# Weight gradient on one core: six phases over eight PSUM banks, slice 0 through hardware queues, results stored from SP

## The chip, the cores and the metric

The kernel runs on one core of a Trainium2 chip. The metric is the device time of one launch in microseconds. The kernel before takes 190.88 us (median of three runs, 190.75 to 191.67).

## What is computed

```python
batch, m, k, n = 16, 512, 1024, 768
input:       (batch, m, k) float32
grad_output: (batch, m, n) float32

grad_weight = np.einsum('bmk,bmn->kn', input, grad_output)   # (1024, 768) float32
```

Batch and m together are 8192 rows that are summed over. The result is X^T G with X of 8192 x 1024 and G of 8192 x 768.

## The kernel before

The 8192 rows are cut into 64 slices of 128 rows (one row for each partition). The 1024 columns of X are eight blocks of 128, numbered k = 0 to 7; the 768 columns of G are a wide part of 512 and a narrow part of 256. One slice therefore needs 16 matmuls: for each k a wide one (128x512, one PSUM bank of 2 KB a partition) and a narrow one (128x256). Over 64 slices that is 512 wide and 512 narrow matmuls, in bf16 with float32 accumulation.

**Loads.** All loads stand on the queue of GpSimd (POOL), which rounds float32 to bf16 on the way. Slice 0 comes in four DMAs (`load_first_slice`, L77 to L80: wide G, two halves of X, narrow G), slice 1 in three (L91 to L93), and slices 2 to 63 in 31 pairs of two DMAs, first G (384 KB in bf16, L107), then X (512 KB, L108). A pair is usable when its X has landed. POOL has eight completion semaphores for its DMAs, taken in turn, so that a DMA is issued only when the one eight places earlier has landed. X and G have 18 buffers each for pairs.

**Order of the work on PE.** The slices fall into chunks of 4, 6, 9, 12, 16 and 17 (`CHUNKS`). Within a chunk, PE takes each slice as it comes and does six of its wide matmuls (seven in the first chunk) into open banks (L209, tiles `st`). The rest of a chunk, two wide blocks and eight narrow ones, is its backlog: it is done group by group during the next chunk (`do_backlog_group`, L151, tile `pb`), two groups before the next chunk's first slice and the others spread between its slices. A program written out in this order is what PE runs; it never changes it. So between two slices of a chunk PE has backlog to do, for data that landed long ago. Warm-up matmuls on a constant tile run ahead of the first slice and four short ones behind each of the first eight slices (L61).

**Adding up.** At a chunk's end the banks are copied (first chunk) or added into `acc` in SBUF: three banks by one DVE add each (L230, L232), a backlog group by one add (L162) or, in the second chunk, a copy on ACT (L160).

**Stores.** Eleven DMAs on POOL's queue: six wide blocks in one DMA of 1536 KB (L234), then each group of the last backlog, two wide and eight narrow, as it is added (L164).

Of the kernel before, what the change touches and what calls it, by code (L numbers as in the profile page):

```python
# [1 line left out]

# [4 lines left out]

CHUNKS = [4, 6, 9, 12, 16, 17]
R_MAIN = 2
WARMUP_MM = 8
FILLER_MM = 4
FILLER_SLICES = 8


@with_exitstack
def kernel(
# [4 lines left out]
    out: bass.AP,  # L24
):
    nc = tc.nc
    P = 128

    B, M, K = input.shape
    _, _, N = grad_output.shape  # L30
    BM = B * M
    S = BM // P
    KSUB = K // P
    NA = 512
    NB = N - NA

    assert sum(CHUNKS) == S

    bf16 = mybir.dt.bfloat16
    f32 = mybir.dt.float32  # L40
# [5 lines left out]
    x_pool = ctx.enter_context(tc.tile_pool(name="x_pool", bufs=18))  # L46
    g_pool = ctx.enter_context(tc.tile_pool(name="g_pool", bufs=18))
    acc_pool = ctx.enter_context(tc.tile_pool(name="acc_pool", bufs=1))
    warm_pool = ctx.enter_context(tc.tile_pool(name="warm_pool", bufs=1))
    ps_pool = ctx.enter_context(tc.tile_pool(name="ps_pool", bufs=2, space=bass.MemoryType.PSUM))  # L50
    pb_pool = ctx.enter_context(tc.tile_pool(name="pb_pool", bufs=2, space=bass.MemoryType.PSUM))
# [5 lines left out]
    wps = pb_pool.tile([P, NA], f32, name="pb")

    def dummy_matmuls(count, width):
        for i in range(count):  # L60
            nc.tensor.matmul(  # L61
                wps[:, :width],
                warm[:, 0:P],
                warm[:, 0:width],
                start=(i == 0),
                stop=(i == count - 1),
            )

    dummy_matmuls(WARMUP_MM, NA)

    slice_aps = [None] * S

    def load_first_slice():
        xa = x_pool.tile([P, NA], bf16, name="xta", bufs=1)
        xb = x_pool.tile([P, NA], bf16, name="xtb", bufs=1)
        gt = g_pool.tile([P, N], bf16, name="gt1", bufs=2)
        nc.gpsimd.dma_start(out=gt[:, 0:NA], in_=G[0:P, 0:NA])  # L77
        nc.gpsimd.dma_start(out=xa, in_=X[0:P, 0:NA])  # L78
        nc.gpsimd.dma_start(out=xb, in_=X[0:P, NA:K])  # L79
        nc.gpsimd.dma_start(out=gt[:, NA:N], in_=G[0:P, NA:N])  # L80
        xparts = [xa, xa, xa, xa, xb, xb, xb, xb]

        def x_ap(k):
            return xparts[k][:, (k % 4) * P : (k % 4 + 1) * P]

        slice_aps[0] = (x_ap, gt)

    def load_single_slice(s):
        xt = x_pool.tile([P, K], bf16, name="xt1", bufs=1)
        gt = g_pool.tile([P, N], bf16, name="gt1", bufs=2)  # L90
        nc.gpsimd.dma_start(out=gt[:, 0:NA], in_=G[s * P : (s + 1) * P, 0:NA])  # L91
        nc.gpsimd.dma_start(out=xt, in_=X[s * P : (s + 1) * P, :])
        nc.gpsimd.dma_start(out=gt[:, NA:N], in_=G[s * P : (s + 1) * P, NA:N])  # L93

        def x_ap(k, xt=xt):
            return xt[:, k * P : (k + 1) * P]

        slice_aps[s] = (x_ap, gt)

    def load_super(first_slice):  # L100
        R = R_MAIN
        s0 = first_slice
        xt = x_pool.tile([P, R, K], bf16, name="xt4")
        gt = g_pool.tile([P, R, N], bf16, name="gt4")
        x_src = X[s0 * P : s0 * P + P * R, :].rearrange("(p r) k -> p r k", r=R)
        g_src = G[s0 * P : s0 * P + P * R, :].rearrange("(p r) n -> p r n", r=R)
        nc.gpsimd.dma_start(out=gt, in_=g_src)  # L107
        nc.gpsimd.dma_start(out=xt, in_=x_src)  # L108
        for j in range(R):

            def x_ap(k, xt=xt, j=j):
                return xt[:, j, k * P : (k + 1) * P]

            slice_aps[s0 + j] = (x_ap, gt[:, j, :])

    assert (S - 2) % R_MAIN == 0
    next_trigger_slice = 0

    def emit_triggers(upto):
        nonlocal next_trigger_slice  # L120
        while next_trigger_slice < min(upto, S):
            s = next_trigger_slice
            if s == 0:
                load_first_slice()
                next_trigger_slice = 1
            elif s == 1:
# [6 lines left out]
    def backlog_regions(ci):
        if ci == 0:
            return [(7, 0, NA)] + [(k, NA, NB) for k in range(KSUB)]
        regions = []
        regions.append((6, 0, NA))
        regions.append((7, 0, NA))
        for k in range(6):
            regions.append((k, NA, NB))  # L140
        regions.append((6, NA, NB))
        regions.append((7, NA, NB))
        return regions

    def do_backlog_group(region, slices, first_chunk, final):
        ksub, nstart, width = region
        pb = pb_pool.tile([P, NA], f32, name="pb")
        n_t = len(slices)
        for j, s in enumerate(slices):
            x_ap, gt = slice_aps[s]  # L150
            nc.tensor.matmul(  # L151
                pb[:, :width],
                x_ap(ksub),
                gt[:, nstart : nstart + width],
                start=(j == 0),
                stop=(j == n_t - 1),
            )
        dst = acc[:, ksub, nstart : nstart + width]
        if first_chunk:
            nc.scalar.copy(out=dst, in_=pb[:, :width])  # L160
        else:
            nc.vector.tensor_add(out=dst, in0=pb[:, :width], in1=dst)  # L162
        if final:
            nc.gpsimd.dma_start(  # L164
                out=OUT[:, ksub, nstart : nstart + width],
                in_=dst,
            )

    prev_slices = []
    slice_idx = 0  # L170
    n_chunks = len(CHUNKS)

    for ci, C in enumerate(CHUNKS):
        first = ci == 0
        last = ci == n_chunks - 1

        chunk_slices = list(range(slice_idx, slice_idx + C))
        slice_idx += C

        if ci + 1 < n_chunks:  # L180
            emit_triggers(slice_idx + CHUNKS[ci + 1])
        else:
            emit_triggers(S)

        n_stream = 7 if first else 6

        st0 = ps_pool.tile([P, 3, NA], f32, name="st")
        st1 = ps_pool.tile([P, 3, NA], f32, name="st")
        sts = [st0[:, 0], st0[:, 1], st0[:, 2], st1[:, 0], st1[:, 1], st1[:, 2]]
        extra = []  # L190
        if first:
            extra = [pb_pool.tile([P, NA], f32, name="pb")]
            sts += extra

        groups = backlog_regions(ci - 1) if ci > 0 else []
        n_groups = len(groups)
        gi = 0

        for i in range(C):
            if C > 1:  # L200
                quota = 2 + (i * max(0, n_groups - 2)) // (C - 1)
            else:
                quota = n_groups
            while gi < n_groups and gi < quota:
                do_backlog_group(groups[gi], prev_slices, ci - 1 == 0, False)
                gi += 1
            x_ap, gt = slice_aps[chunk_slices[i]]
            for k in range(n_stream):
# [61 lines left out]
```

## Time and profile before

| | |
|---|---|
| Median of three runs | 190.88 us |
| Profiled execution, first to last instruction (span) | 189.0 us |
| PE busy | 173.4 us, 92% of the span |
| DVE, POOL, ACT busy | 43.6, 43.1, 6.3 us |
| DMA traffic of the core | 32.66 MB, of which loads to about 143 us |
| Groups on PE with most time | L209 wide matmuls 89.0 us, L151 wide and narrow 88.9 us |
| Last matmul's add starts on DVE | 180.42 us |
| Last store issued on POOL | 181.14 us |

The profile has no time of its own for the profiled execution besides its span; the median stands 1.9 us above the span, which is launch and end around it. Busy PE time is the sum of matmul records whose ends are modelled; the pitch from one matmul to the next is read from the chain of waits, where a row gives the time of a run of matmuls and their count. "DMA share" in a table of stretches is the busy share of the 16 DMA engines; it goes above 1 where packets overlap. GB/s counts bytes written: a load that rounds float32 to bf16 reads twice what is counted.

### The profile page before, as it was taken

What the parts mean: (1) busy time and instruction counts of PE and PEld (TensorE: products, weight loads), DVE (VectorE), ACT (ScalarE), POOL (GpSimd) and SP (SyncE); (2) the same over time, 40 slices, a digit from 0 to 9 for tenths busy, and PEclk for the clock granted to TensorE, in tenths of its full rate; (3) what the DMA queues carried; (4) which work ended last, traced back from release to release, by engine and by line L of the source; (5) the groups of instructions that cost most, each with busy time, mean ns of one, the idle gap of its engine ahead of it and who ended that gap; (6) DMA issues with size and microseconds to landing.
All of it is one profiled execution on the core that took longest, in us unless ns stands there. A gap on an engine that the chain in (4) does not pass through costs nothing.

```text
span 189.0 us, 2417 instructions
## 1 busy us (share of the span) xinstructions
PE 173.4 (92%) x1064; PEld 102.9 (54%) x1064; DVE 43.6 (23%) x65; ACT 6.3 (3%) x13; POOL 43.1 (23%) x84
## 2 busy tenths in 40 slices
PE   6658989999999999999999999999999999999910
PEld 2134545565546566545566564466666665488810
DVE  1002203712370111550001108210000007231200
ACT  2003321000000000000000000000000000000000
POOL 7732222322222222222222204221000000223210
PEclk9999999999999999999999999999999999999995
DMA  4999999999999999999999999999994000571210
GB/s 61 138 210 214 212 215 213 212 215 212 212 214 210 213 214 211 214 215 211 215 213 212 213 212 212 213 214 212 214 213 80 3 0 0 189 283 63 79 56 0
DMA packets 10890, 32.66 MB, mean 173 GB/s; under 512 B 1280, under 2 KB 2048, under 8 KB 10880
## 3 DMA queue, kind: packets, MB, share of 16 engines
q0 software_dynamic: 10880, 32.51, 84.2%
q8 instruction: 8, 0.13, 0.3%
q14 instruction: 2, 0.02, 0.0%
HBM read 58.72 MB, written 3.15 MB: 327 GB/s over the span
## 4 chain that ended last, share of the span: by engine, by line
PE 68%; DMA 13%; issue 9%; POOL 5%; DVE 1%; POOLq 0%; DVEq 0%
PE st L209 38%; PE pb L151 30%; DMA xt<-in_input_dram 13%; POOL out_dram L164 3%; DVE acc L232 1%; POOL out_dram L234 0%; POOL gt L77 0%; POOLq L265 0%; POOL xta L78 0%; POOL gt L80 0%; POOL xtb L79 0%; POOL gt L107 0%; POOL gt L91 0%; POOLq L164 0%; DVE acc L230 0%
## 5 line engine op out<-in xcount | busy, mean ns | idle before, releaser
L209 PE MATMUL st<-gt,xt 128*128 128x512 bf16 x378 | 89.0, 379 | 4.7 <-DMA xt<-in_input_dram 4.7
L151 PE MATMUL pb<-gt,xt 128*128 128x256 bf16 (+1 forms) x627 | 88.9, 293 | 0.0
L151 PEld LDWEIGHTS <-xt 128*128 128x128 bf16 x627 | 61.3, 98 | 28.0 <-issue 0.2
L209 PEld LDWEIGHTS <-xt 128*128 128x128 bf16 x381 | 37.0, 98 | 41.9 <-DMA xt<-in_input_dram 5.6
L162 DVE TENSOR_TENSOR acc<-pb,acc 128x256 f32<-128x256 f32 (+1 forms) x50 | 23.8, 477 | 107.8 <-PE pb L151 107.8
L108 POOL DMA_DIRECT2D xt<-in_input_dram x31 | 16.5, 533 | 46.4 <-DMA xt<-in_input_dram 45.6
L107 POOL DMA_DIRECT2D gt<-in_grad_output_dram x31 | 16.6, 535 | 44.4 <-DMA gt<-in_grad_output_dram 33.8
L230 DVE TENSOR_TENSOR acc<-st,acc 128x1536 f32<-128x1536 f32 x5 | 8.8, 1758 | 12.2 <-PE st L209 12.2
L232 DVE TENSOR_TENSOR acc<-st,acc 128x1536 f32<-128x1536 f32 x5 | 8.7, 1747 | 0.0
L164 POOL DMA_DIRECT2D out_dram<-acc x10 | 5.4, 542 | 13.8 <-DVE acc L162 13.8
L234 POOL DMA_DIRECT2D out_dram<-acc x1 | 0.9, 852 | 32.9 <-DVE acc L232 32.9
L61 PE MATMUL pb<-warm 128*128 128x128 bf16 (+1 forms) x40 | 5.9, 301 | 1.5 <-DVE warm L56 1.5
L227 DVE COPY acc<-st 128x512 f32<-128x512 f32 x3 | 2.0, 684 | 16.3 <-PE st L209 16.3
L61 PEld LDWEIGHTS <-warm 128*128 128x128 bf16 x40 | 3.1, 106 | 3.8 <-issue 1.7
L160 ACT COPY acc<-pb 128x256 f32<-128x256 f32 (+1 forms) x9 | 3.5, 396 | 9.1 <-PE pb L151 9.0
L225 ACT COPY acc<-st 128x512 f32<-128x512 f32 x3 | 1.6, 594 | 15.1 <-PE st L209 15.1
L209 PE MATMUL st<-gt,xta 128*128 128x512 bf16 x4 | 1.5, 512 | 0.1
L151 PE MATMUL pb<-gt,xtb 128*128 128x256 bf16 (+1 forms) x5 | 1.5, 293 | 0.1
L225 ACT ACT_TABLE_LOAD x1 | 1.3, 1283 | 0.7 <-PEq L254 0.7
L209 PEld LDWEIGHTS <-xta 128*128 128x128 bf16 x4 | 0.4, 130 | 1.6 <-DMA xta<-in_input_dram 1.0
L209 PE MATMUL st<-gt,xtb 128*128 128x512 bf16 x2 | 0.6, 384 | 0.6 <-DMA xtb<-in_input_dram 0.6
L209 PE MATMUL pb<-gt,xt 128*128 128x512 bf16 x3 | 1.1, 379 | 0.0
(18 smaller groups left out, 8.2 us busy)
## 6 DMA issues: line engine op xcount, KB each, us to landing
xt<-in_input_dram POOLq DMA_DIRECT2D x31, 512.0 KB, 17.0
gt<-in_grad_output_dram POOLq DMA_DIRECT2D x31, 384.0 KB, 16.9
out_dram<-acc POOLq DMA_DIRECT2D x1, 1536.0 KB, 6.1
out_dram<-acc POOLq DMA_DIRECT2D x8, 128.0 KB, 2.0
out_dram<-acc POOLq DMA_DIRECT2D x2, 256.0 KB, 4.1
gt<-in_grad_output_dram POOLq DMA_DIRECT2D x2, 128.0 KB, 3.9
xt<-in_input_dram POOLq DMA_DIRECT2D x1, 256.0 KB, 6.0
xta<-in_input_dram POOLq DMA_DIRECT2D x1, 128.0 KB, 3.2
```

The source lines that it names most:

```text
L61: nc.tensor.matmul(wps[:, :width], warm[:, 0:P], warm[:, 0:width], start=(i == 0), stop=(i == count - 1),)
L107: nc.gpsimd.dma_start(out=gt, in_=g_src)
L108: nc.gpsimd.dma_start(out=xt, in_=x_src)
L151: nc.tensor.matmul(pb[:, :width], x_ap(ksub), gt[:, nstart : nstart + width], start=(j == 0), stop=(j == n_t - 1),)
L160: nc.scalar.copy(out=dst, in_=pb[:, :width])
L162: nc.vector.tensor_add(out=dst, in0=pb[:, :width], in1=dst)
L164: nc.gpsimd.dma_start(out=OUT[:, ksub, nstart : nstart + width], in_=dst,)
L209: nc.tensor.matmul(sts[k], x_ap(k), gt[:, 0:NA], start=(i == 0), stop=(i == C - 1),)
L225: nc.scalar.copy(out=acc[:, b, 0:NA], in_=st0[:, b, :])
L227: nc.vector.tensor_copy(out=acc[:, 3 + b, 0:NA], in_=st1[:, b, :])
L230: nc.vector.tensor_add(out=dst0, in0=st0[:, :, :], in1=dst0)
L232: nc.vector.tensor_add(out=dst1, in0=st1[:, :, :], in1=dst1)
```

## The change

The kernel is written anew with the same tiling into slices, blocks k and wide and narrow parts.

- **Phases.** The slices fall into phases of 4, 8, 10, 14, 18 and 10 (`PHASES`). All eight wide banks are open in a phase. The first slices of a phase are streamed (slice by slice, eight wide matmuls each); the last 1, 2, 4, 6, 10 and 10 of it (`BANKWISE`) are done bank by bank: for k = 0 all these slices, then the bank is added into `acc`, then k = 1. Behind that come the eight narrow blocks of the same phase, each over all slices of the phase. Nothing of a phase is left for the next. One pool of eight banks serves all.
- **Slice 0** is loaded as float32 by three DMAs of 256 KB on the hardware queues of SP (two) and ACT (one), and rounded on the chip by three copies on DVE and two on ACT. Its narrow part and those of slices 1 to 3 come in one DMA on POOL's queue (`gn`, 512 pieces of 256 columns); slices 1 to 3 come one by one (wide G, X); slices 4 to 63 in 30 pairs as before, now with 20 buffers.
- **Adding up** is one bank at a time: in the first phase copies that alternate between DVE and ACT, later adds on DVE alone.
- **Stores** are 16 DMAs on SP's queue, one behind each add of the last phase.
- **Warm-up** is 20 matmuls of 128 columns; the short matmuls between slices are gone.

```diff
-CHUNKS = [4, 6, 9, 12, 16, 17]
+PHASES = [4, 8, 10, 14, 18, 10]
+BANKWISE = [1, 2, 4, 6, 10, 10]
+WARMUP = 20
...
+    nc.sync.dma_start(out=g0f, in_=G[0:P, 0:NA])
+    nc.scalar.dma_start(out=x0f[:, 0:NA], in_=X[0:P, 0:NA])
+    nc.sync.dma_start(out=x0f[:, NA:K], in_=X[0:P, NA:K])
...
+    nc.vector.tensor_copy(out=g0, in_=g0f)
+    nc.scalar.copy(out=x0[0], in_=x0f[:, 0:256])
+    nc.vector.tensor_copy(out=x0[1], in_=x0f[:, 256:512])
+    nc.vector.tensor_copy(out=x0[2], in_=x0f[:, 512:768])
+    nc.scalar.copy(out=x0[3], in_=x0f[:, 768:1024])
...
+    for s in range(1, C0):
...
+        nc.gpsimd.dma_start(out=gt, in_=G[s * P : (s + 1) * P, 0:NA])
+        nc.gpsimd.dma_start(out=xt, in_=X[s * P : (s + 1) * P, :])
...
+    nc.gpsimd.dma_start(
+        out=gn, in_=G[0 : C0 * P, NA:N].rearrange("(s p) n -> p s n", p=P)
+    )
...
+        if last:
+            nc.sync.dma_start(out=OUT[:, k, c0:c1], in_=dst)
...
+        streamed = slices[: C - BANKWISE[ph]]
+        rest = slices[C - BANKWISE[ph] :]
+        if streamed:
+            banks = [psum.tile([P, NA], f32, name="bank") for _ in range(KS)]
+            for i, s in enumerate(streamed):
+                for k in range(KS):
+                    nc.tensor.matmul(
+                        banks[k], xblk[s](k), gwide[s], start=(i == 0), stop=False
+                    )
+        for k in range(KS):
+            bank = banks[k] if streamed else psum.tile([P, NA], f32, name="bank")
+            for i, s in enumerate(rest):
+                nc.tensor.matmul(
+                    bank,
+                    xblk[s](k),
+                    gwide[s],
...
+            evacuate(acc[:, k, 0:NA], bank, first, last, k, 0, NA)
+        for k in range(KS):
+            bank = psum.tile([P, NA], f32, name="bank")
+            for i, s in enumerate(slices):
+                nc.tensor.matmul(
+                    bank[:, 0:NB],
+                    xblk[s](k),
+                    gnarrow[s],
...
+            evacuate(acc[:, k, NA:N], bank[:, 0:NB], first, last, k, NA, N)
...
-        if last:
-            nc.gpsimd.dma_start(out=OUT[:, 0:6, 0:NA], in_=acc[:, 0:6, 0:NA])
```

**Where slices 52 and 53 are first used, on PE.** The order of before, in the last chunk (slices 47 to 63). `xt4_681` and `gt4_682` are the pair of slices 50 and 51, `xt4_685` and `gt4_686` the pair 52 and 53; "waits DMASW" is a wait for a load.

```order
L209 MATMUL st_950<-gt4_682,xt4_681 128x512
L209 LDWEIGHTS xt4_681
L209 MATMUL st_950<-gt4_682,xt4_681 128x512
L209 LDWEIGHTS xt4_685 [waits DMASW2_49]
L209 MATMUL st_949<-gt4_686,xt4_685 128x512 [waits DMASW1_49]
L209 LDWEIGHTS xt4_685
```

The order of after, in the fifth phase (slices 36 to 53), on PE where its bank-wise part begins: `xt_645` is the pair 42 and 43, `xt_649` 44 and 45, `xt_661` 50 and 51, `xt_665` 52 and 53; `bank_944` is k = 0, `bank_945` k = 1.

```order
L139 MATMUL bank_951<-gt_644,xt_645 128x512
L145 LDWEIGHTS xt_649 [waits DMASW0_49]
L145 MATMUL bank_944<-gt_648,xt_649 128x512 [waits DMASW7_49]
...
L145 LDWEIGHTS xt_661 [waits DMASW6_49]
L145 MATMUL bank_944<-gt_660,xt_661 128x512 [waits DMASW5_49]
L145 LDWEIGHTS xt_661
L145 MATMUL bank_944<-gt_660,xt_661 128x512
L145 LDWEIGHTS xt_665 [waits DMASW0_49]
L145 MATMUL bank_944<-gt_664,xt_665 128x512 [waits DMASW7_49]
L145 LDWEIGHTS xt_665
L145 MATMUL bank_944<-gt_664,xt_665 128x512
L145 LDWEIGHTS xt_649
L145 MATMUL bank_945<-gt_648,xt_649 128x512
```

Before, six matmuls of slice 51 stand between the waits for two pairs, and backlog between slices 50 and 51 and between 52 and 53. After, the waits for the last five pairs of the phase stand four matmuls apart, all ahead of the second bank.

**The head of POOL's queue.** The first nine DMAs of before, on POOL:

```order
L77 DMA gt1_87<-in_grad_output_dram 128x512
L78 DMA xta_85<-in_input_dram 128x512
L79 DMA xtb_86<-in_input_dram 128x512
L80 DMA gt1_87<-in_grad_output_dram 128x256
L91 DMA gt1_93<-in_grad_output_dram 128x512
L92 DMA xt1_92<-in_input_dram 128x1024
L93 DMA gt1_93<-in_grad_output_dram 128x256
L107 DMA gt4_98<-in_grad_output_dram 128x1536
L108 DMA xt4_97<-in_input_dram 128x2048
```

The first nine of after, on POOL:

```order
L81 DMA gw1_106<-in_grad_output_dram 128x512
L82 DMA x1_107<-in_input_dram 128x1024
L81 DMA gw2_110<-in_grad_output_dram 128x512
L82 DMA x2_111<-in_input_dram 128x1024
L81 DMA gw3_114<-in_grad_output_dram 128x512
L82 DMA x3_115<-in_input_dram 128x1024
L86 DMA gn_118<-in_grad_output_dram 128x4x256
L96 DMA gt_120<-in_grad_output_dram 128x1536
L97 DMA xt_121<-in_input_dram 128x2048
```

The last two of before bring slices 2 and 3, the last two of after slices 4 and 5. Three slices come one by one where one pair and one single slice did, and slice 0 has left the queue but for its narrow part.

## Rows read from the trace of the kernel before

**Rows 1.** The profile's page: the span, and busy time of each engine.

```profile
span 189.0 us, 2417 instructions
...
PE 173.4 (92%) x1064; PEld 102.9 (54%) x1064; DVE 43.6 (23%) x65; ACT 6.3 (3%) x13; POOL 43.1 (23%) x84
```

**Rows 2.** Stretches: from:to in us, busy us (instructions) by engine, PEclk, DMA share, GB/s.

```profile
core 0: us, PE busy (x) PEld busy (x) DVE busy (x) ACT busy (x) POOL busy (x), PEclk, DMA share, GB/s
...
30.00:40.00 10.00, 10.00 (x59) 5.52 (x58) 5.47 (x6) 0.74 (x2) 2.64 (x5) 1.00 1.07 213
145.00:150.00 5.00, 5.00 (x32) 3.04 (x31) 0.42 (x1) 0.00 (x0) 0.00 (x0) 1.00 0.00 0
```

**Rows 3.** The chain of waits: start us, us, what, with the count of matmuls.

```profile
122.21 2.59 PE st L209 x12
124.80 1.75 PE pb L151 x16
...
130.88 2.59 PE st L209 x12
```

**Rows 4.** The timeline, PE: start us, us, engine, line, operation; in brackets idle before.

```profile
28.51 1.47 PE L209 MATMUL st<-gt,xt 128*128 128x512 bf16 x6 [1.09 <-DMA xt<-in_input_dram]
```

**Rows 5.** The timeline, POOL: X loads issued when an earlier X load had landed.

```profile
28.75 0.53 POOL L108 DMA_DIRECT2D xt<-in_input_dram  x1 [1.69 <-DMA xt<-in_input_dram]
...
54.63 0.53 POOL L108 DMA_DIRECT2D xt<-in_input_dram  x1 [1.93 <-DMA xt<-in_input_dram]
...
84.82 0.53 POOL L108 DMA_DIRECT2D xt<-in_input_dram  x1 [1.66 <-DMA xt<-in_input_dram]
...
123.86 0.53 POOL L108 DMA_DIRECT2D xt<-in_input_dram  x1 [1.67 <-DMA xt<-in_input_dram]
```

**Rows 6.** The timeline, first us: ACT, POOL, PE and its weight loads.

```profile
0.74 1.28 ACT L225 ACT_TABLE_LOAD   x1 [0.74 <-PEq L254]
...
1.25 0.67 POOL L77 DMA_DIRECT2D gt<-in_grad_output_dram  x1 [0.81 <-POOLq L254]
...
1.46 3.59 PE L61 MATMUL pb<-warm 128*128 128x512 bf16 x8 [1.46 <-DVE warm L56]
5.19 1.47 PE L209 MATMUL st<-gt,xta 128*128 128x512 bf16 x4
...
5.60 0.15 PEld L209 LDWEIGHTS <-xta 128*128 128x128 bf16 x1 [0.27 <-issue]
6.02 0.14 PEld L209 LDWEIGHTS <-xta 128*128 128x128 bf16 x1 [0.28 <-issue]
```

**Rows 7.** DMA totals of two stretches: 2 to 10 us, then 30 to 140 us.

```profile
DMA packets 1046, 1.04 MB, mean 130 GB/s; under 512 B 111, under 2 KB 879, under 8 KB 1046
...
DMA packets 7326, 23.41 MB, mean 213 GB/s; under 512 B 814, under 2 KB 814, under 8 KB 7319
```

**Rows 8.** Stretches of one us: loads at the start, then the large store.

```profile
2.00:3.00 1.00, 1.00 (x4) 0.31 (x3) 0.00 (x0) 0.02 (x1) 1.00 (x3) 1.00 0.48 48
3.00:4.00 1.00, 1.00 (x4) 0.31 (x3) 0.00 (x0) 0.00 (x0) 1.00 (x3) 1.00 1.00 146
...
163.00:164.00 1.00, 1.00 (x6) 0.49 (x5) 0.00 (x0) 0.00 (x0) 0.45 (x1) 1.00 0.98 377
```

**Rows 9.** The end: timeline, waits of SP's queue, and stores from issue to landing.

```profile
180.42 0.42 DVE L162 TENSOR_TENSOR acc<-pb,acc 128x256 f32<-128x256 f32 x1 [1.43 <-PE pb L151]
181.14 0.54 POOL L164 DMA_DIRECT2D out_dram<-acc  x1 [1.32 <-DVE acc L162]
...
SPq L265 <- PEq L265: 5.6, 2, 5.2
...
out_dram<-acc POOLq DMA_DIRECT2D x8, 128.0 KB, 2.0
```

**Rows 10.** Groups by shape: DVE adds, busy us and mean ns of one, idle before.

```profile
L162 DVE TENSOR_TENSOR acc<-pb,acc 128x256 f32<-128x256 f32 x40 | 17.0, 425 | 98.1 <-PE pb L151 98.1
...
L162 DVE TENSOR_TENSOR acc<-pb,acc 128x512 f32<-128x512 f32 x10 | 6.8, 687 | 9.6 <-PE pb L151 9.6
```

More of the change, by code (lines that the diff above doesn't have):

```diff
@@ L26 @@
     nc = tc.nc
-    P = 128
+    bf16 = mybir.dt.bfloat16
+    f32 = mybir.dt.float32
     B, M, K = input.shape
     _, _, N = grad_output.shape
[L31 to L34, printed above, removed]
+    S = B * M // P
+    KS = K // P
     NB = N - NA
-    assert sum(CHUNKS) == S
-    bf16 = mybir.dt.bfloat16
-    f32 = mybir.dt.float32
+    assert sum(PHASES) == S
     X = input.rearrange("b m k -> (b m) k")
@@ L44 @@
     OUT = out.rearrange("(ks p) n -> p ks n", p=P)
[L46 to L51, printed above, removed]
@@ L53 @@
-    acc = acc_pool.tile([P, KSUB, N], f32)
-    warm = warm_pool.tile([P, NA], bf16)
-    nc.vector.memset(warm, 1.0)
[L57 to L91, printed above, removed]
-        nc.gpsimd.dma_start(out=xt, in_=X[s * P : (s + 1) * P, :])
[L93 to L114, printed above, removed]
@@ L133, in backlog_regions @@
[L133 to L160, printed above, removed]
-        else:
[L162 to L208, printed above, removed]
-                nc.tensor.matmul(
-                    sts[k],
-                    x_ap(k),
-                    gt[:, 0:NA],
@@ new lines @@
+    head = ctx.enter_context(tc.tile_pool(name="head", bufs=1))
+    xg = ctx.enter_context(tc.tile_pool(name="xg", bufs=20))
+    accp = ctx.enter_context(tc.tile_pool(name="accp", bufs=1))
+    psum = ctx.enter_context(tc.tile_pool(name="psum", bufs=8, space=bass.MemoryType.PSUM))
+    acc = accp.tile([P, KS, N], f32, name="acc")
+    xblk = [None] * S
+    gwide = [None] * S
+    gnarrow = [None] * S
+    g0f = head.tile([P, NA], f32, name="g0f")
+    x0f = head.tile([P, K], f32, name="x0f")
@@ new lines @@
+    nc.sync.dma_start(out=g0f, in_=G[0:P, 0:NA])
+    nc.scalar.dma_start(out=x0f[:, 0:NA], in_=X[0:P, 0:NA])
+    nc.sync.dma_start(out=x0f[:, NA:K], in_=X[0:P, NA:K])
+    warm = head.tile([P, P], bf16, name="warm")
+    nc.vector.memset(warm, 1.0)
+    wps = psum.tile([P, NA], f32, name="bank")
+    for i in range(WARMUP):
+        nc.tensor.matmul(wps[:, 0:P], warm, warm, start=(i == 0), stop=(i == WARMUP - 1))
+    g0 = head.tile([P, NA], bf16, name="g0")
+    x0 = [head.tile([P, 256], bf16, name=f"x0_{i}") for i in range(4)]
@@ new lines @@
+    nc.vector.tensor_copy(out=g0, in_=g0f)
[3 more added lines that the diff above has]
+    nc.scalar.copy(out=x0[3], in_=x0f[:, 768:1024])
+    xblk[0] = lambda k: x0[k // 2][:, (k % 2) * P : (k % 2 + 1) * P]
+    gwide[0] = g0[:, :]
+    C0 = PHASES[0]
+    for s in range(1, C0):
+        gt = head.tile([P, NA], bf16, name=f"gw{s}")
+        xt = head.tile([P, K], bf16, name=f"x{s}")
+        nc.gpsimd.dma_start(out=gt, in_=G[s * P : (s + 1) * P, 0:NA])
+        nc.gpsimd.dma_start(out=xt, in_=X[s * P : (s + 1) * P, :])
+        xblk[s] = lambda k, xt=xt: xt[:, k * P : (k + 1) * P]
+        gwide[s] = gt[:, :]
@@ new lines, with load_pair @@
+    gn = head.tile([P, C0, NB], bf16, name="gn")
+    nc.gpsimd.dma_start(
+        out=gn, in_=G[0 : C0 * P, NA:N].rearrange("(s p) n -> p s n", p=P)
+    )
+    for s in range(C0):
+        gnarrow[s] = gn[:, s, :]
+    def load_pair(s):
+        gt = xg.tile([P, 2, N], bf16, name="gt")
+        xt = xg.tile([P, 2, K], bf16, name="xt")
+        rows = slice(s * P, (s + 2) * P)
+        nc.gpsimd.dma_start(out=gt, in_=G[rows, :].rearrange("(p r) n -> p r n", r=2))
+        nc.gpsimd.dma_start(out=xt, in_=X[rows, :].rearrange("(p r) k -> p r k", r=2))
+        for r in range(2):
+            xblk[s + r] = lambda k, xt=xt, r=r: xt[:, r, k * P : (k + 1) * P]
+            gwide[s + r] = gt[:, r, 0:NA]
+            gnarrow[s + r] = gt[:, r, NA:N]
@@ new lines, with load_upto, evacuate @@
+    loaded = C0
+    def load_upto(n):
+        nonlocal loaded
+        while loaded < min(n, S):
+            load_pair(loaded)
+            loaded += 2
+    evac_count = 0
+    def evacuate(dst, src, first, last, k, c0, c1):
+        nonlocal evac_count
+        if first:
+            if evac_count % 2 == 0:
+                nc.vector.tensor_copy(out=dst, in_=src)
+            else:
+                nc.scalar.copy(out=dst, in_=src)
+            evac_count += 1
+        else:
+            nc.vector.tensor_add(out=dst, in0=src, in1=dst)
+        if last:
+            nc.sync.dma_start(out=OUT[:, k, c0:c1], in_=dst)
@@ new lines @@
+    s0 = 0
+    for ph, C in enumerate(PHASES):
+        first, last = ph == 0, ph == len(PHASES) - 1
+        slices = list(range(s0, s0 + C))
+        s0 += C
+        load_upto(s0 + (PHASES[ph + 1] if not last else 0))
+        streamed = slices[: C - BANKWISE[ph]]
[10 more added lines that the diff above has]
+            for i, s in enumerate(rest):
+                nc.tensor.matmul(
+                    bank,
+                    xblk[s](k),
+                    gwide[s],
+                    start=(i == 0 and not streamed),
+                    stop=(i == len(rest) - 1),
+                )
+            evacuate(acc[:, k, 0:NA], bank, first, last, k, 0, NA)
[6 more added lines that the diff above has]
+                    gnarrow[s],
```

39 lines of the change are left out of this document (2 added, 37 removed).

## The prediction

> **What bounds the kernel now.** I read the page first, then the table of stretches, then the chain of waits, then the places where PE waits. The span is 189.0 us and PE is busy for 173.4 of it [rows 1]; the median of the runs, 190.88, lies 1.9 above the span, and I carry that over unchanged. The stretches show two limits side by side. From 30 to 40 us PE is full and the DMA engines are full too, at 213 GB/s written; at 145 to 150 PE is still full and no load is left [rows 2]. So the loads are only a little faster than PE, and which of the two is late depends on the place.
>
> PE's price comes from the chain: 12 wide matmuls take 2.59 us, 0.2158 each, and 16 narrow ones 1.75 us, 0.1093 each [rows 3]. A slice is 8 of both, 2.60 us; the whole product is 512 of both, 166.4 us. A pair of slices lands every 4.31 us: between the loads released at 28.75 and 54.63 lie six pairs [rows 5], so 2.16 us a slice. The wide part of a slice alone is 1.73 us. **A stretch of PE that does only wide matmuls of fresh slices is faster than the loads, and one that does both kinds is slower.** The rest follows from this.
>
> Before, PE waits for a load for the last time at 28.51 us, for slices 8 and 9 [rows 4]. What is left then: 456 wide and 488 narrow matmuls (the last two slices of the second chunk, two narrow groups of the first chunk, the second chunk's own backlog, 54 whole slices), 98.4 + 53.3 = 151.7 us, which ends at 180.2. The last add starts on DVE at 180.42 [rows 9]. So the pitches hold, and behind 28.51 PE loses nothing. In the fifth and sixth chunks it is far behind the loads. The load of slices 52 and 53 had landed at 123.6: POOL's next X load on that semaphore is issued at 123.86, and PE took slice 8 at 28.51 where POOL followed at 28.75 [rows 4, 5], so I take 0.24 off. PE comes to slice 52 in the middle of the run at 130.88, at 132.2 [rows 3], 8.6 us after it landed.
>
> **Part by part: the phases.** The matmuls are the same 512 and 512. What moves is how soon PE asks for a slice. I walk through the phases with the arrivals of before. Slices 10 and 11 land one pair behind 28.51, at 32.8. Behind that phase 1 has 16 wide and 64 narrow matmuls, 10.5 us, and ends at 43.3. Phase 2 streams six slices (10.4 us) and does two slices of the first bank (0.4), and is at 54.1 when it asks for slices 20 and 21, which land at 54.4 [rows 5]. It then has 30 wide and 80 narrow, 15.2 us, and ends at 69.6. Phase 3 streams eight slices (13.8), does four of the first bank (0.9), and asks at 84.3 for slices 34 and 35, which land at 84.6 [rows 5]; 44 wide and 112 narrow, 21.7 us, end it at 106.3. **Phase 4** streams eight (13.8), does eight slices of the first bank (1.7), and asks at 121.9 for slices 52 and 53. They land at 123.6 [rows 5]. PE runs in order, so seven banks of work that is ready stand behind this wait of 1.7 us. After it come 72 wide (15.5) and 144 narrow (15.7), and phase 5, whose data are long there, with 80 and 80 (26.0): 57.3 us, which ends at 180.9. Before ended at 180.2 by the same pitches: **+0.7 us**, with the arrivals unchanged. All waits on the way sum to some 5.7 us (about 3.4 in phase 1, 0.3, 0.3, 1.7). Whatever happens in the first microseconds on PE, DVE or ACT is hidden up to that: the copies that round slice 0, its later start than 5.19 [rows 6], the dummies that go. Only a shift of the loads themselves moves the end, and it moves it one for one.
>
> **The loads' shift.** I price DMA work per engine from two stretches [rows 7]. In 2 to 10 us data flow for some 7.5 us (the share of the third microsecond is 0.48 [rows 8]): 16 x 7.5 = 120 engine-us for 1046 packets and 1.04 MB. In 30 to 140: 1760 for 7326 and 23.41 MB. Both hold with 0.058 us a packet and 0.057 us for 1000 bytes written. Slices 0 to 3 before: nine DMAs, 81 packets with their completion ones and 114.7 KB an engine, 4.70 + 6.54 = 11.24 us. After, on POOL's queue: seven DMAs, 87 packets and 90.1 KB, 5.05 + 5.14 = 10.18. To this come the three float32 loads of slice 0, 0.786 MB that no row shows. Their nearest row is the float32 store, 377 GB/s [rows 8]: 2.09 us. Bounds: at the bytes that the pair stream reads, 2 x 213 GB/s, 1.85; with the price of POOL's packets of 2 KB, 2.97. With 2.09 the loads end 1.03 us later. Against it, SP and ACT issue earlier: ACT is released at 0.74, POOL's first DMA starts at 1.25 [rows 6] and its data flow at about 2.5. If a hardware queue needs the same 1.25 us from issue to data, the engines work from 2.0, 0.5 us earlier; bounds 0 and 1.0. So the shift is 1.03 - 0.5 = **+0.5 us**, between -0.2 and +1.9.
>
> The Trainium skill ("DMA: Bandwidth & Descriptors", section "Issuing engines are not separate DMA queues") says that DMAs of all issuing engines run on the same 16 engines and that issuing from several saves only the issue time. The share of 1.00 already in the fourth microsecond [rows 8] agrees: the engines are what is short. Held strictly, the head start is worth nothing and the sum 0.5 higher. Its section "Latency and other measured facts" gives about 0.6 us to the first byte on a hardware queue against 1 us on GpSimd's; an estimate from that puts the first byte near 1.4 and the sum 0.6 lower. No run here shows either.
>
> **Adds, banks, buffers.** From phase 1 on DVE does 8 wide adds of 0.687 and 8 narrow of 0.425 [rows 10], 8.9 us a phase. The tightest place is phase 1, where banks finish every 0.43 us: the eighth is free 5.5 us behind the first, while PE asks for it 9.5 us in, behind seven narrow groups. Nothing; uncovered it would be a few tenths. The buffers that 20 pairs share are free before the load that needs them (phases 1 and 2 end at 43 and 70). Nothing.
>
> **The end.** Both kernels end with a narrow group, an add of 0.42 and a store. Before, POOL starts the store 0.30 us behind the add, writes descriptors for 0.54, and it lands 2.0 us after the start; then SP's queue sees 5.6 us of closing waits [rows 9], which I keep. A store issued by SP saves between nothing and all of 0.30 + 0.54; I take half, **-0.4**. The other 15 stores go out beside matmuls: 256 KB at 377 GB/s is 0.7 us for each 2.2.
>
> **Sum:** 190.88 + 0.7 + 0.5 - 0.4 = **191.7 us**. With the bounds: 190.88 + 0.7 - 0.2 - 0.84 = 190.5 to 190.88 + 0.7 + 1.9 = 193.5. A change of this kernel within 0.5%, 0.95 us, can hardly be told from none, so this counts as the same, near the upper edge.
>
> **Rivals.** (A) *The hardware queues add work and no time*: the head start is lost because the first three DMAs only push POOL's back, and their packets cost what POOL's cost. Shift 1.0 to 1.9, time 192.2 to 193.1, slower. It decides from a shift of 0.65. For it: the full engines. Against it: the engines are idle until 2.5.
> (B) *PE's clock*. PE starts in the lower level: weight loads 0.42 us apart for 512 columns, at 5.60 and 6.02 [rows 6], are 1.2 GHz. Before, warm-up runs until slice 0 comes; after, 20 short matmuls of about 0.11 us are over near 3.4 and slice 0, loaded and then rounded, comes near 6. If the level stays low through phase 0, 10.4 us of matmuls take twice that; some 7.7 of it fall into waits (5.7 and about 2 in phase 0), the rest, 2.7, adds: 194.4. The Trainium skill ("TensorE: Matmul & The Clock Gate", "HAM oscillation") states that a long idle gap returns the clock to the lower level; before, the gaps of PE are covered by dummies, so no row shows it.
> (C) *Three queues hide each other's packet cost.* If the head flows at the pair stream's rate, slices 0 to 3 take 1.835 MB / 213 GB/s = 8.6 us instead of 11.24: shift -3.1 with the head start, time 188.1, faster. It decides from -1.25. Against it: a share of 1.00 at only 146 GB/s [rows 8].
> That slice 0 is not early at all is possible and costs nothing, by the waits above.
>
> **How the numbers follow.** Forecast (shift -1.25 to 0.65) 0.48, A 0.37, B 0.06, C 0.09. So slower 0.43, same 0.48, faster 0.09. The range goes from 190.2 to 193.2: the bounds of the sum, with the far ends of A and most of B and C left out.
>
> **What would show it.** In the profile after: PE waits for an X load near 122 to 124 us, for 1 to 2 us, and for none later; the last add starts 57.5 us behind it; smaller waits near 54 and 84; loads end 0 to 1.5 us later than 143. Wrong would be: no wait in phase 4, waits of PE for DVE, GB/s in the pair stream other than 213, or a closing wait other than 5.6 us.

## The result, and the profile after

The changed kernel takes **184.22 us** (median of four runs) against 190.96 for the kernel before, measured beside it: a ratio of 0.9645, 95% interval 0.9612 to 0.9678, some 6.7 us. One of the four runs, 186.6 us, was slow, and the ratio leaves it out. The forecast was 191.7 us, within the noise of no change, range 190.2 to 193.2. It missed, and for the larger part by a mechanism that was not among its rivals.

The page of the changed kernel, against [rows 1]:

```profile
span 182.0 us, 2421 instructions
...
PE 171.2 (94%) x1032; PEld 102.2 (56%) x1044; DVE 49.1 (27%) x92; ACT 5.6 (3%) x11; POOL 36.1 (20%) x71
```

The span fell by 7.0 us. To see where, I cut it at the start of the last add on DVE. The timeline of the end and the waits of SP's own queue, after (start or total us, us or count, operation), answer to [rows 9]:

```profile
178.61 0.42 DVE L122 TENSOR_TENSOR acc<-bank,acc 128x256 f32<-128x256 f32 x1 [0.67 <-PE bank L156]
...
SPq L189 <- DMA out_dram<-acc: 1.0, 1, 1.0
...
SPq L189 <- PEq L189: 0.7, 2, 0.5
...
out_dram<-acc SPq DMA_DIRECT2D x8, 128.0 KB, 1.7
```

Before, the last add started at 180.42 and the span ended 8.6 us later; after, 178.61 and 3.4 us later. So 1.8 us are won ahead of the last add and **5.2 behind it**. Of those 5.2, 4.9 are one row: the closing wait of SP's queue is 0.7 us where it was 5.6.

Ahead of the last add, the loads. POOL's X load that waits for the X of slices 52 and 53, and PE at that place, after (timeline), against [rows 5]:

```profile
121.37 0.53 POOL L97 DMA_DIRECT2D xt<-in_input_dram  x1 [1.71 <-DMA xt<-in_input_dram]
...
121.14 15.71 PE L145 MATMUL bank<-gt,xt 128*128 128x512 bf16 x71 [1.46 <-DMA xt<-in_input_dram]
136.69 15.88 PE L156 MATMUL bank<-gt,xt 128*128 128x256 bf16 x144
152.41 17.43 PE L145 MATMUL bank<-gt,xt 128*128 128x512 bf16 x78
169.67 8.90 PE L156 MATMUL bank<-gt,xt 128*128 128x256 bf16 x80
```

PE waits 1.5 us for slices 52 and 53 in phase 4, then runs without a wait to its end, 57.5 us later at the last add. That is the place, the size and the rest that the prediction worked out. But the slices land 2.5 us sooner than before (121.37 for 123.86), where the prediction had them 0.5 later. The stretches of the first microseconds (columns as in [rows 2]), against [rows 8]:

```profile
2.00:3.00 1.00, 1.00 (x12) 1.00 (x11) 0.00 (x0) 0.45 (x1) 1.00 (x3) 1.00 0.80 213
3.00:4.00 1.00, 0.37 (x4) 0.10 (x1) 0.00 (x0) 0.00 (x0) 1.00 (x3) 1.00 0.95 346
4.00:5.00 1.00, 0.02 (x1) 0.02 (x2) 0.67 (x2) 0.40 (x1) 1.00 (x3) 1.00 1.14 302
...
7.00:8.00 1.00, 1.00 (x4) 0.35 (x3) 0.00 (x0) 0.00 (x0) 0.21 (x1) 1.00 1.19 216
```

Two of the same stretches before, which [rows 8] does not have:

```profile
4.00:5.00 1.00, 1.00 (x3) 0.14 (x1) 0.00 (x0) 0.00 (x0) 1.00 (x3) 1.00 1.14 121
...
7.00:8.00 1.00, 0.76 (x5) 0.41 (x6) 0.00 (x0) 0.00 (x0) 0.52 (x1) 1.00 0.89 151
```

From 2 to 4 us only the float32 loads move data, 213 and 346 GB/s; from 4 to 5 they and POOL's queue together move 302. POOL's queue alone had moved 48, 146 and 121 before. These rates count what is written; counted by what is read, POOL's are twice as high, 96, 292 and 242, and a float32 load's stay as they are. Behind the float32 loads, from 7 to 8 us, POOL's queue moves 216 GB/s where it had moved 151. The pair stream itself is unchanged at 213.

### The profile page after: what moved, and what is told of

It is laid out like the page before. It is cut to its first block, busy times and chain, and to the rows that moved or that the text cites. A ratio compares the mean times of both kernels' runs of the same rounds, so it can differ in the third digit from the quotient of the medians.

```text
span 182.0 us, 2421 instructions
## 1 busy us (share of the span) xinstructions
PE 171.2 (94%) x1032; PEld 102.2 (56%) x1044; DVE 49.1 (27%) x92; ACT 5.6 (3%) x11; POOL 36.1 (20%) x71
## 4 chain that ended last, share of the span: by engine, by line
DMA 62%; PE 31%; POOL 3%; issue 2%; DVE 0%; POOLq 0%
DMA xt<-in_input_dram 62%; PE bank L145 18%; PE bank L156 13%; POOL gw L81 1%; POOL x L82 1%; POOL gn L86 0%; POOL gt L96 0%; DVE acc L122 0%; POOLq L178 0%
## 5 line engine op out<-in xcount | busy, mean ns | idle before, releaser
L122 DVE TENSOR_TENSOR acc<-bank,acc 128x512 f32<-128x512 f32 (+1 forms) x80 | 43.8, 557 | 117.6 <-PE bank L145 84.4
L145 PE MATMUL bank<-gt,xt 128*128 128x512 bf16 x251 | 56.3, 379 | 2.7 <-DMA xt<-in_input_dram 2.3
L156 PE MATMUL bank<-gt,xt 128*128 128x256 bf16 x480 | 53.2, 273 | 0.0
L139 PE MATMUL bank<-gt,xt 128*128 128x512 bf16 x218 | 48.9, 379 | 2.0 <-DMA xt<-in_input_dram 1.7
L156 PEld LDWEIGHTS <-xt 128*128 128x128 bf16 x480 | 47.0, 98 | 6.5
L145 PEld LDWEIGHTS <-xt 128*128 128x128 bf16 x256 | 24.7, 98 | 33.4 <-DMA xt<-in_input_dram 4.4
L139 PEld LDWEIGHTS <-xt 128*128 128x128 bf16 x224 | 21.8, 98 | 27.6 <-DMA xt<-in_input_dram 2.5
L117 DVE COPY acc<-bank 128x512 f32<-128x512 f32 (+1 forms) x8 | 4.1, 553 | 8.1 <-PE bank L145 7.2
L139 PEld LDWEIGHTS <-x 128*128 128x128 bf16 x24 | 2.8, 119 | 6.0 <-issue 2.8
L139 PE MATMUL bank<-g,x 128*128 128x512 bf16 x8 | 3.6, 631 | 1.6 <-ACT x L69 1.6
L139 PE MATMUL bank<-gw,x 128*128 128x512 bf16 x16 | 4.0, 408 | 0.0
L119 ACT COPY acc<-bank 128x512 f32<-128x512 f32 (+1 forms) x8 | 3.5, 486 | 9.0 <-PE bank L145 7.4
L156 PE MATMUL bank<-gn,x 128*128 128x256 bf16 x32 | 3.7, 272 | 0.0
L156 PEld LDWEIGHTS <-x 128*128 128x128 bf16 x32 | 3.1, 98 | 0.6
L145 PE MATMUL bank<-gw,x 128*128 128x512 bf16 x7 | 1.8, 379 | 0.1
```

Source lines behind the costliest of these rows:

```text
L117: nc.vector.tensor_copy(out=dst, in_=src)
L119: nc.scalar.copy(out=dst, in_=src)
L122: nc.vector.tensor_add(out=dst, in0=src, in1=dst)
L139: nc.tensor.matmul(banks[k], xblk[s](k), gwide[s], start=(i == 0), stop=False)
L145: nc.tensor.matmul(bank, xblk[s](k), gwide[s], start=(i == 0 and not streamed), stop=(i == len(rest) - 1),)
L156: nc.tensor.matmul(bank[:, 0:NB], xblk[s](k), gnarrow[s], start=(i == 0), stop=(i == C - 1),)
```

## The experiments

Two theories. **Theory 1**: the closing wait follows a store that POOL's queue issues near the end. **Theory 2**: all loads come earlier because the hardware queues cover a slow start of POOL's queue. The runs are named e1 to e11, as their expectations name them. And the prediction's own term for the phases, +0.7 us, and its wait in phase 4 were put to the test.

### The closing wait

All 16 stores on POOL's queue (run e1):

```diff
-            nc.sync.dma_start(out=OUT[:, k, c0:c1], in_=dst)
+            nc.gpsimd.dma_start(out=OUT[:, k, c0:c1], in_=dst)
```

> The changed kernel (184.2 us) with its 16 stores on POOL's queue instead of SP's. Theory 1 (the closing wait of SP's queue follows a store that POOL issued near the end): the wait is 5.6 us again instead of 0.7 and the last store lands some 0.3 us later, about 189.4 us, the last add unchanged at 178.6. Rival (the closing wait comes from something else in the kernel of before, its open banks or its backlog, not from the stores): closing wait 0.7, about 184.6 us.

Measured 189.53 us, ratio to before 0.9952 (0.9936 to 0.9967). The last add stands at 178.81, as in the changed kernel. Waits of SP's queue, this kernel:

```profile
SPq L189 <- PEq L189: 5.8, 2, 5.3
```

The queue of the stores alone is worth 5.3 us of the 6.7 by the medians (measured on two chips), 5.7 by the spans (187.7 for 182.0). One store of 16 on POOL, the last (run e2):

```diff
-            nc.sync.dma_start(out=OUT[:, k, c0:c1], in_=dst)
+            queue = nc.gpsimd if (k == KS - 1 and c0 == NA) else nc.sync
+            queue.dma_start(out=OUT[:, k, c0:c1], in_=dst)
```

> The changed kernel with only the last of the 16 stores on POOL's queue, the others on SP's. If one store of POOL just before the end is enough for the long closing wait: 5.6 us of wait, about 189.4 us. If the wait grows with the number of stores that POOL issued: 0.7 to 1.5 us of wait, 184.5 to 185.5 us.

Measured 188.49 us, ratio 0.9893 (0.9853 to 0.9932). The same row of this kernel:

```profile
SPq L190 <- PEq L190: 4.5, 2, 4.0
```

One late store is enough for most of it. The profile is of an execution of 190.82 us, not of the median: there PE waited 1.98 us for slices 52 and 53, its granted clock was 0.50 from 124 to 126 us, and the last add came at 181.37. The closing wait lies behind all that. The eight wide stores on POOL, the eight narrow ones, which come last, on SP (run e11):

```diff
-            nc.sync.dma_start(out=OUT[:, k, c0:c1], in_=dst)
+            queue = nc.gpsimd if c0 == 0 else nc.sync
+            queue.dma_start(out=OUT[:, k, c0:c1], in_=dst)
```

> The changed kernel with the eight wide stores of the last phase on POOL's queue and the eight narrow ones, the last, on SP's: POOL's last DMA is then issued some 9 us ahead of the end. If the closing wait counts from POOL's last DMA: 0.7 us, 184.2 us. If any store of POOL calls for it: about 5 us, 189 us.

Measured 184.14 us, ratio 0.9655 (0.9613 to 0.9697). The same row of this kernel, and POOL's last store (timeline):

```profile
SPq L190 <- PEq L190: 0.7, 2, 0.5
...
171.46 0.54 POOL L125 DMA_DIRECT2D out_dram<-acc  x1 [1.62 <-DVE acc L122]
```

Eight stores of POOL cost nothing here, where the last of them is issued 11.1 us ahead of the span's end (182.6). In the kernel of before, e1 and e2 the span ends 7.9, 8.2 and 7.0 us behind POOL's last issue. So the wait is not for stores as such, nor for their number. The rows fit a wait that counts from POOL's last DMA and is hidden when work runs on long enough; a wait that comes only when the very last DMA of all is POOL's would give the same rows, and no run separates the two. And the kernel of before with nothing but its 11 stores moved to SP (run e3):

```diff
-            nc.gpsimd.dma_start(
+            nc.sync.dma_start(
                 out=OUT[:, ksub, nstart : nstart + width],
...
-            nc.gpsimd.dma_start(out=OUT[:, 0:6, 0:NA], in_=acc[:, 0:6, 0:NA])
+            nc.sync.dma_start(out=OUT[:, 0:6, 0:NA], in_=acc[:, 0:6, 0:NA])
```

> The kernel of before with its 11 stores on SP's queue, nothing else. Theory 1: the last add stays at 180.4, the closing wait falls from 5.6 to 0.7 us and the store lands 0.3 us earlier, about 185.7 us. Rival (the wait belongs to the rest of that kernel): about 190.6 us.

Measured 184.83 us against 190.53 beside it, ratio 0.9714 (0.9678 to 0.9749). Its last add and the closing wait (timeline, waits of SP's queue):

```profile
180.44 0.42 DVE L162 TENSOR_TENSOR acc<-pb,acc 128x256 f32<-128x256 f32 x1 [1.43 <-PE pb L151]
...
SPq L265 <- PEq L265: 0.7, 2, 0.5
```

PE, DVE and the loads are where they were (180.42 before), and 5.7 us are gone. Theory 1 stands in both directions. What the chip does in those 5 us is not told by any row.

### The head of the loads

The changed kernel with slice 0 back on POOL's queue (run e4):

```diff
...
-    nc.sync.dma_start(out=g0f, in_=G[0:P, 0:NA])
-    nc.scalar.dma_start(out=x0f[:, 0:NA], in_=X[0:P, 0:NA])
-    nc.sync.dma_start(out=x0f[:, NA:K], in_=X[0:P, NA:K])
...
+    nc.gpsimd.dma_start(out=g0, in_=G[0:P, 0:NA])
+    nc.gpsimd.dma_start(out=x0[0], in_=X[0:P, 0:NA])
+    nc.gpsimd.dma_start(out=x0[1], in_=X[0:P, NA:K])
...
```

> The changed kernel with slice 0 loaded and rounded by three DMAs at the head of POOL's queue, as in the kernel of before; the copies on DVE and ACT are gone. Theory 2 (the loads of the whole kernel come earlier because the hardware queues start the DMA engines sooner and let POOL write ahead): slices 52 and 53 land at 123.6 to 125.5 us instead of 121.1, the last add moves from 178.6 by as much, 186.7 to 188.6 us. Rival (the head is quick by its form, slices one by one and one DMA for the narrow parts): 184 to 185 us.

Measured 185.66 us, ratio 0.9747 (0.9713 to 0.9782). POOL's X load behind slices 52 and 53, the last add, and two stretches of the start of this kernel:

```profile
123.95 0.53 POOL L90 DMA_DIRECT2D xt<-in_input_dram  x1 [1.72 <-DMA xt<-in_input_dram]
...
181.18 0.42 DVE L115 TENSOR_TENSOR acc<-bank,acc 128x256 f32<-128x256 f32 x1 [0.67 <-PE bank L149]
...
4.00:5.00 1.00, 0.00 (x0) 0.00 (x0) 0.00 (x0) 0.00 (x0) 1.00 (x3) 1.00 0.86 99
...
10.00:12.00 2.00, 2.00 (x10) 0.75 (x9) 0.00 (x0) 0.00 (x0) 1.10 (x3) 1.00 1.16 206
```

The loads land as late as in the kernel of before (123.86), and the last add moves with them from 178.61 to 181.18: the two 2.6 us are the same. The time moved by less than that (1.4 us between the medians of two chips, 2.2 between the spans): 185.66 lies below the 186.7 to 188.6 of Theory 2 and above the 184 to 185 of its rival, and it is the landing of the loads that decides for Theory 2. The last stretch shows what the prediction had wrong: from 10 to 12 us this kernel loads single slices, short packets, at 206 GB/s. Short packets are slow only at the start. So the next run (e5) sends long ones first:

```diff
+    load_pair(4)
     nc.gpsimd.dma_start(out=g0, in_=G[0:P, 0:NA])
     nc.gpsimd.dma_start(out=x0[0], in_=X[0:P, 0:NA])
...
-    loaded = C0
+    loaded = C0 + 2
```

> The kernel of e4 (slice 0 on POOL's queue, 185.7 us, slices 52 and 53 landed at 123.7) with the pair 4 and 5 moved to the head of POOL's queue, so that the first packets are long ones (3 and 4 KB) and the short ones come later. Theory 2a (short packets as such cost more, 0.058 us each): same bytes and packets, slices 52 and 53 land at 123.7 again, PE starts some 4 us later, which its waits hide, 185 to 186.5 us. Theory 2b (the first six us of POOL's queue are slow whatever their packets are, because the engines start on a queue that has nothing written ahead; later short packets flow at over 190 GB/s): the short packets now flow behind the pair; if long packets suffer less in the slow start, 52 and 53 land at 121.5 to 122.5, 183.5 to 184.5 us; if the slow start costs the same time, 123.7.

Measured 184.57 us, ratio 0.9697 (0.967 to 0.9723). POOL's X load behind slices 52 and 53; two stretches; and the DMA totals from 9 to 10 us, of this kernel:

```profile
122.68 0.53 POOL L61 DMA_DIRECT2D xt<-in_input_dram  x1 [1.72 <-DMA xt<-in_input_dram]
...
3.00:4.00 1.00, 0.37 (x4) 0.10 (x1) 0.00 (x0) 0.00 (x0) 1.00 (x3) 1.00 0.97 147
4.00:5.00 1.00, 0.00 (x0) 0.00 (x0) 0.00 (x0) 0.00 (x0) 1.00 (x3) 1.00 1.08 211
...
DMA packets 217, 0.20 MB, mean 198 GB/s; under 512 B 24, under 2 KB 217, under 8 KB 217
```

The same bytes in as many packets land 1.3 us sooner, only because their order changed. In the tenth microsecond 217 packets, all short, pass at 198 GB/s: 16 engine-us / 217 = 0.074 us each, where the prediction priced 0.058 + 0.057 = 0.115 for 1 KB. Theory 2b holds, with the landing in its range and the time at the upper edge of it: the start of POOL's queue is slow, for about 2 us with long packets and 7 to 8 with short ones (e4 and the kernel of before), and later short packets flow at nearly the full rate. Why the start is slow is open. That POOL has not written enough ahead is one reading; the trace of e4 does not support it, since by 5 us POOL had issued six DMAs of 0.92 MB together, of which 0.28 MB had moved. Nor does any run load slice 0 through one hardware queue instead of two. PE started at 10.08 us here, 5.1 later than in the changed kernel, and the span grew by 1.0, no more than its loads are late: the waits that the prediction put at 5.7 us hide this start.

### The phases

To leave out the phases alone, slice 0's wide parts in the kernel of before went to the hardware queues, first without (run e6) and then with the stores on SP (run e7):

```diff
-        nc.gpsimd.dma_start(out=gt[:, 0:NA], in_=G[0:P, 0:NA])
-        nc.gpsimd.dma_start(out=xa, in_=X[0:P, 0:NA])
-        nc.gpsimd.dma_start(out=xb, in_=X[0:P, NA:K])
...
+        nc.sync.dma_start(out=g0f, in_=G[0:P, 0:NA])
+        nc.scalar.dma_start(out=x0f[:, 0:NA], in_=X[0:P, 0:NA])
+        nc.sync.dma_start(out=x0f[:, NA:K], in_=X[0:P, NA:K])
+        nc.vector.tensor_copy(out=gt[:, 0:NA], in_=g0f)
+        nc.scalar.copy(out=xa, in_=x0f[:, 0:NA])
+        nc.vector.tensor_copy(out=xb, in_=x0f[:, NA:K])
```

> The kernel of before with only its slice 0 (wide G and X) on the hardware queues as float32, rounded by two copies on DVE and one on ACT. Theory 2: every later load lands some 2.5 us sooner (52 and 53 at 121.1 instead of 123.6), PE's last wait at 26.0 instead of 28.5, and since PE of this kernel waits no more behind that, its end moves by the same 2.5: 188.1 us. Rival (the gain of the loads is no gain here, since PE is limited by its own work): 190.5 us.

> The kernel of before with slice 0 on the hardware queues and the stores on SP, so that of the change only the phases (and the adds bank by bank) are left out. By the prediction's term for the phases, +0.7 us for the change, this is 0.7 us faster than the changed kernel: the last add at 177.9, 183.0 to 183.5 us. Rival (the phases themselves bring time, e.g. by shorter adds at the end): 184.5 us or more.

Measured 190.78 us, ratio 1.0018 (0.9988 to 1.0048), and 186.84 us, ratio 0.9817 (0.9791 to 0.9844), both about 3 us above what was expected, and both test something else than was meant: with slice 0 rounded into the tile that its narrow part is loaded into, the builder put the load of slice 1's wide G behind the pair 2 and 3 on POOL's queue. PE, and two stretches, of the second:

```profile
12.86 2.72 PE L214 MATMUL st<-gt,xt 128*128 128x512 bf16 x6 [4.78 <-DMA gt<-in_grad_output_dram]
...
14.00:16.00 2.00, 2.00 (x6) 0.73 (x5) 0.00 (x0) 0.00 (x0) 0.69 (x2) 0.50 1.08 217
...
20.00:24.00 4.00, 3.88 (x30) 2.29 (x29) 2.48 (x4) 1.71 (x4) 0.76 (x3) 1.00 1.07 212
```

PE stood still for 4.8 us, and then its granted clock is 0.50 from 14 to 16 us, the level of 1.2 GHz: six wide matmuls take 2.72 us where [rows 4] has 1.47. It is back at 1.00 by 20. In this order of work PE has no waits later in which that could hide. The idle stretch that lowers the clock is what the Trainium skill ("TensorE: Matmul & The Clock Gate", "HAM oscillation — how this bites in real kernels") describes; here the trace shows it. With tiles of its own for slice 0, POOL's queue keeps its order (run e9):

```diff
+        gw = g_pool.tile([P, NA], bf16, name="gw0", bufs=1)
+        gn = g_pool.tile([P, NB], bf16, name="gn0", bufs=1)
...
-        nc.vector.tensor_copy(out=gt[:, 0:NA], in_=g0f)
+        nc.vector.tensor_copy(out=gw, in_=g0f)
...
-        nc.gpsimd.dma_start(out=gt[:, NA:N], in_=G[0:P, NA:N])
+        nc.gpsimd.dma_start(out=gn, in_=G[0:P, NA:N])
...
```

> The kernel of e7 again, with slice 0 in tiles of its own, so that POOL's queue keeps its order: in e7 the load of slice 1's wide G had moved behind the pair 2 and 3, PE stood still for 4.8 us and its clock then fell to the lower level. Now only the phases of the change are left out. By the prediction's +0.7 us for the phases: last add near 177.9, 183.0 to 183.5 us, against 184.2 for the changed kernel. Rival (this kernel's order gains nothing from earlier loads): as the kernel of before with stores on SP, 184.8 us.

Measured 183.51 us, ratio 0.963 (0.9576 to 0.9683). POOL's X load behind slices 52 and 53, and the last add, of this kernel:

```profile
121.15 0.53 POOL L121 DMA_DIRECT2D xt<-in_input_dram  x1 [1.67 <-DMA xt<-in_input_dram]
...
177.70 0.42 DVE L175 TENSOR_TENSOR acc<-pb,acc 128x256 f32<-128x256 f32 x1 [1.43 <-PE pb L164]
```

The same loads (121.15 for 121.37), the old order of work: the last add is 0.9 us sooner than with the phases, 0.7 of it beyond the loads. This kernel's own end is set by PE's work, whose last wait for a load is at 16.64 us, so the term reads 0.7 to 0.9. This kernel also keeps the old warm-up and short matmuls, the loads of slices 1 to 3 and the eleven stores, so of the change it leaves out these too, and not the phases alone. A second pair of runs, e4 and e3, has slice 0 on POOL's queue and the stores on SP's in both: the last add comes at 181.18 with the phases and 180.44 without, with slices 52 and 53 landing 0.3 us later (123.95 and 123.66), and the times are 185.66 and 184.83 us. The term of the prediction holds in the trace, at 0.4 to 0.9 us; in time the two kernels can't be told apart (0.963 and 0.9645, intervals overlap). **The phases, as the change sizes them, brought nothing; moving the stores and slice 0 to other queues brought all of it.**

### The wait in phase 4

Shorter bank-wise parts in phases 2, 3 and 4, counted from 0 (run e8):

```diff
-BANKWISE = [1, 2, 4, 6, 10, 10]
+BANKWISE = [1, 2, 2, 2, 2, 10]
```

> The changed kernel with BANKWISE = [1, 2, 2, 2, 2, 10] instead of [1, 2, 4, 6, 10, 10]: PE asks for the last slices of phases 2, 3 and 4 later. Theory 3 (the wait for 52 and 53 and the two small ones before it are on the path): PE waits no more behind 30.5 us, the rest from there is 145.5 us, the last add moves from 178.6 to 176.3, 181.9 us. Rival (the adds, 0.69 us for a bank that now takes 0.43, become late and hold PE at the narrow blocks): 184 us or more.

Measured **181.55 us**, ratio 0.9544 (0.9518 to 0.9569). PE in phase 4 of this kernel, and the last add:

```profile
103.56 27.79 PE L139 MATMUL bank<-gt,xt 128*128 128x512 bf16 x128
131.19 3.62 PE L145 MATMUL bank<-gt,xt 128*128 128x512 bf16 x16
...
176.56 0.42 DVE L122 TENSOR_TENSOR acc<-bank,acc 128x256 f32<-128x256 f32 x1 [0.67 <-PE bank L156]
```

PE now asks for slices 52 and 53 at 131 us and has no wait behind the one for slices 10 and 11. The last add comes 2.05 us sooner (178.61 to 176.56), the waits of phases 2, 3 and 4 in all. Next, the early waits, with smaller first phases (run e10):

```diff
-PHASES = [4, 8, 10, 14, 18, 10]
-BANKWISE = [1, 2, 4, 6, 10, 10]
+PHASES = [4, 4, 6, 10, 14, 16, 10]
+BANKWISE = [1, 2, 2, 2, 2, 2, 10]
```

> The changed kernel with PHASES = [4, 4, 6, 10, 14, 16, 10] and BANKWISE = [1, 2, 2, 2, 2, 2, 10]: against e8 (181.55) only the early phases are cut smaller, so that narrow blocks fill PE's waits for slices 8 to 11. Walked through with the arrivals of the changed kernel: 2.3 us of waits go, the last add near 174.2, 179.3 us. Rival (eight adds of 0.69 and eight of 0.43 us on DVE do not fit into a phase of four slices, 10.4 us of PE with 9 of adds, and hold the banks of the next phase): 1.2 us of it comes back, 180.5 us, with PE waiting for DVE near 28 to 31 us.

Measured **179.84 us**, ratio 0.9431 (0.9382 to 0.9479). PE in the first phases, and the last add, of this kernel:

```profile
21.89 3.63 PE L145 MATMUL bank<-gt,xt 128*128 128x512 bf16 x16 [0.88 <-DMA xt<-in_input_dram]
25.35 3.66 PE L156 MATMUL bank<-gt,xt 128*128 128x256 bf16 x32
28.84 7.07 PE L139 MATMUL bank<-gt,xt 128*128 128x512 bf16 x31
...
174.64 0.42 DVE L122 TENSOR_TENSOR acc<-bank,acc 128x256 f32<-128x256 f32 x1 [0.67 <-PE bank L156]
```

One wait for a load is left behind the start, and none for DVE. The last add and the time are 0.4 and 0.5 us above the 174.2 and 179.3 that were expected, and no row says why. It is faster than both kernels of the case, by 4.4 us than the change.

## Why the prediction was wrong, and where it was right

**The closing wait: the step that failed most.** The prediction kept "5.6 us of closing waits" as a constant around the kernel and weighed only the last store's own path, where it took 0.4 us. The store gave 0.3; the wait gave 4.9. The row was there [rows 9], with SP's queue waiting for another sequencer for 5.6 us when all data had landed; nothing in the kernel before showed whose it was. A wait with no shown cause that stands behind an operation which the change moves to another queue should have been a term with bounds of 0 and 5.6, and a rival of its own.

**The loads' shift: the second step that failed, in size and sign.** Predicted +0.5 (-0.2 to +1.9), measured -2.5. The price of 0.058 us a packet came from fitting two stretches that differ in more than packet size: one is the first 8 us of POOL's queue, the other its steady stream. e5 and e4 show short packets at 198 and 206 GB/s later on; the low rate belongs to the start. Nor did a DMA share of 1.00 at 146 GB/s show that the engines could carry no more: POOL's queue alone had a share of 0.86 at 99 GB/s and 1.16 at 206 in e4. Counted in bf16 bytes, the changed kernel had moved 0.50 MB by 5 us (slice 0, half of its 0.78 MB of float32, and 0.11 of POOL's) for 0.32 before, and from 5 to 10 us 1.01 for 0.72: 0.18 and 0.29 MB, at 213 GB/s 0.9 and 1.3 us of the 2.5. Rival C, with 0.09, had the result of this ("the head flows at the pair stream's rate", shift -3.1), but laid it to three queues that hide each other's packet cost; e4 and e5 reach nearly that rate on one queue, later in the program. Rival A was right that the first DMAs push POOL's back (in the change POOL's queue moves nothing until 4 us, before until 2.6) and wrong in what followed: from 5 us POOL's queue ran at 190 to 216 GB/s. The head start of 0.5 us taken in the sum was within its bounds but small: the first bytes flow at 1.7 us, where POOL's flowed at 2.6.

The Trainium skill's sentence ("DMA: Bandwidth & Descriptors", "Issuing engines are not separate DMA queues"), that issuing from several engines only saves issue time, led toward rival A. On the steady stream no run here tests it: in both kernels it stands on POOL's queue alone, at 213 GB/s. At the start of the kernel the trace does not agree: with slice 0 on the queues of SP and ACT the loads land 2.5 us sooner (the change against e4), and there the measurement decides.

**The phases: right.** PE's wait for slices 52 and 53 (1.5 us for 1.7), the 57.5 us behind it, +0.7 us against the old order (0.4 to 0.9 by e9 and e4), waits that hide the start (e5). PE never waits for an add of DVE; one load of G waits 1.6 us for its buffer, and the X loads behind it land in step. Given the landing of the loads, the last add comes within 0.2 us of where this working puts it, in the change, e4, e8 and e9, and 0.4 us later in e10.

**Rival B** was half there: PE's first eight wide matmuls take 3.6 us, 0.45 each where [rows 3] gives 0.2158, and the waits hid it. The profile's column reads 1.00 there, so that this is the lower clock is argued from the pace and not shown. In e7, where the order of work has no later waits, the stall and the granted clock of 0.50 behind it put the last add at 181.90, 4.2 us behind that of e9.

The low end of the predicted range, 190.2, lies below the sum's own bound of 190.5, and no term gives it; nothing turns on that.

## What to carry to other kernels

Read the end of the trace behind the last useful instruction as a stage of its own: a DMA on GpSimd's queue that is issued last can hold the closing for 5 us, and one on SP's costs 0.7. Do not fit a price from two stretches that differ in their place in the program; look for the same operation at another time of the same trace first. Where loads and PE are nearly as fast, walk through every place at which PE asks for fresh data and write down the margin: the negative margins are the gain that is left, and here cost 4.4 us.

## What the runs showed of the hardware

- The closing wait of SP's queue: 5.1 to 5.8 us where all stores come from POOL's queue (the kernel of before, e1, e6), 4.5 with POOL's last store alone (e2), 0.7 where POOL's last DMA was issued 11.1 us ahead of the end (e11) or all stores come from SP's.
- POOL's queue at the start of a kernel: 48 to 172 GB/s for some 7 us with short packets (e4); short packets at 175 to 206 GB/s behind long ones (e5) or later (e4, 206). Float32 loads on hardware queues in the fourth microsecond: 346 GB/s.
- PE idle for 4.8 us (e7): granted clock 0.50 from 12 to 18 us, with PE at work again from 12.86; back at 1.00 by 20.
